# A hybrid layer with a PEER expert mixer: 160 gathered tokens instead of 128, and a down product with stationary weights and a transposed output

## The chip, the cores and the metric

The kernel runs on one core of a Trainium2 chip. A core has five engines that work side by side, each through its own queue of instructions: TensorE (PE) for matrix products, with the loading of its stationary operand shown apart (PEld); VectorE (DVE) and ScalarE (ACT) for elementwise work; GpSimd (POOL), here mostly the issuer of indirect gathers; and SyncE (SP), which issues most of the other transfers. Sixteen DMA engines move the data. The metric is the device time of one execution in microseconds (us); lower is better.

## The reference

One decoder layer on 512 tokens of width 2048, in float32. A mixer (gMLP and mLSTM heads behind one input projection) is added to x; the change does not touch it. Then comes the PEER mixer, in which each token picks 128 of 16384 experts (8 heads x 16), and a final norm:

```
h2 = rmsnorm(x, norm2_g)
qp = h2 @ peer_wq;  s1, s2 = scores of its two halves against 128 keys each
eidx, gate = top 16 of 16 x 16 candidate pairs, softmax, per head
act  = gelu(einsum("td,thkd->thk", h2, peer_u[eidx]))
x    = x + einsum("thk,thkd->td", gate * act, peer_v[eidx])
out  = rmsnorm(x, final_g)
```

## The kernel before

All large products are made from split operands: each float32 value becomes a high part `whi` or `Th` (rounded to fp32r) and a low part `wlo` or `Tl`, and `mm3` (lines 97 to 100) adds three matmuls, high x high, high x low, low x high. `split` (lines 68 to 70) makes the parts, the high one on ScalarE, the low one on VectorE.

The front, up to the last matmul of tile po at 699.8 us, is the mixer. After it, x with the mixer added goes to `x2d` in DRAM, the normed first 128 tokens go to `h2d`, and the normed, transposed activations of all tokens stand in `Th`, `Tl`.

The PEER mixer is computed in two ways at once:

- **The gathered path**, for tokens 0 to 127. `experts()` (line 543) gathers, for each of the 128 picks q, one row of `peer_u` per token (an indirect DMA into a tile `g`, three buffers, line 533), takes its dot product with the token's row `h20` on VectorE (line 548), then the gelu, and then gathers rows of `peer_v` and adds them, scaled, to `acc0` (line 557): 256 gathers of 128 x 2048 values.
- **The dense path**, for tokens 128 to 511. The *up stage* multiplies all 128 blocks of 128 experts by the 384 dense tokens (tile `pu`, line 698: weights stationary, the 384 tokens moving), takes the gelu and stores it as `Ad`. Meanwhile `combine()` (line 614) does the routing of the dense tokens and builds the combination matrix: per token, two one-hot matrices (lines 636 and 638, VectorE) are multiplied (line 639, TensorE, tile `pwb`, float32, each recorded as two matmuls), so that the gates stand at the places of the chosen experts. It is stored as `Wd` in 12 blocks of 32 tokens. The *down stage* goes through 16 groups of 8 expert blocks. `product(g)` loads `Ad` and `Wd` of a group, multiplies them and splits the result into `C`; then the activations of 128 tokens are stationary and 512 columns of `peer_v` move (line 748, tile `pv`): 4 column blocks `ch`, 3 token blocks, 8 expert blocks. `close` (line 751) adds each result to `acc`, which begins as x2.

The order of the work is set in four ways. The weights come in *pieces* of 128 x 1024, two from each 1 MB load on SyncE's queue, split three pieces ahead of their use (`LA = 3`); there are 256 pieces in each stage, 24 up matmuls or 18 down matmuls each. The gathers are handed out by `gather_step` (line 573): a fixed share is owed per piece (the 256 gathers over 466 slots, with 0.45 of the share while the first product is made and over the first 12 down pieces), and `fetch` adds a wait for the last matmul of a piece four back, so that gathers run at TensorE's pace. Units of routing and combination are handed out by a similar count (line 709). Last, the order on each engine's queue is not the order of writing: a scheduler with a model of the times of the instructions sets it when the program is built.

At the end, the last column block of the last group runs token block by token block: sums of squares, `rstd` (line 55), scaling, output (lines 763 to 776). The gathered tokens are finished beside the last group (lines 791 to 800).

Of the kernel before, what the change touches and what calls it, by code (L numbers as in the profile page):

```python
# [27 lines left out]
KP = KD // NP  # L28
TOPK = 16
# [6 lines left out]
def layer(ctx, tc, a, out, dbg=None):  # L36
# [18 lines left out]
    def rstd(dst, ssq, n):  # L55
        m = ssq.shape[-1]
        v = tiny.tile([P, 32], F32, tag="rs_v", name="rs_v")[:, :m]
        r = tiny.tile([P, 32], F32, tag="rs_r", name="rs_r")[:, :m]
        t = tiny.tile([P, 32], F32, tag="rs_t", name="rs_t")[:, :m]
# [362 lines left out]
    h2d = tc.dram_tile([P, D], F32, name="h2d")  # L422
    with ExitStack() as mx:
# [20 lines left out]
        hn = mid.tile([P, D], F32, name="hn")  # L444
        nc.vector.scalar_tensor_tensor(hn, xs[0], r2[:, 0:1], g2, op0=ALU.mult, op1=ALU.mult)
        nc.gpsimd.dma_start(h2d, hn)
# [6 lines left out]
    nc.gpsimd.dma_start(h20, h2d)  # L453
    sel0 = hg.tile([P, 3, P], F32, name="sel0")
    act = hg.tile([P, P], F32, name="act")
    rstack = ExitStack()
# [15 lines left out]
    done = [0]  # L472

    def route(t, heads=range(8), nb=4):
        s = slice(t * P, (t + 1) * P)
        for h0 in range(heads[0], heads[-1] + 1, nb):
# [36 lines left out]
            if t == 0:  # L513
# [3 lines left out]
                nc.vector.tensor_copy(eidx[:, r], ef)  # L517
                done[0] += nb * TOPK
# [7 lines left out]
            nc.vector.tensor_tensor(g3, g3, gs[:, :, None].to_broadcast(flat), op=ALU.mult)  # L526
            yield
# [4 lines left out]
    def fetch(table, q):  # L532
        g = hg.tile([P, D], F32, tag="g", name="g", bufs=3)
        i = nc.gpsimd.indirect_dma_start(out=g, out_offset=None, in_=table,  # L534
                                         in_offset=bass.IndirectOffsetOnAxis(ap=eidx[:, q:q + 1], axis=0))
# [5 lines left out]
    acc0 = []  # L541

    def experts():
        for q in range(P):
            while done[0] <= q:
                yield "wait"
            g = fetch(a["peer_u"], q)
            nc.vector.tensor_tensor_reduce(out=g, in0=h20, in1=g, op0=ALU.mult, op1=ALU.add, scale=1.0,  # L548
                                           scalar=0.0, accum_out=act[:, q:q + 1])
            yield "step"  # L550
        nc.scalar.activation(gate0, act, AF.Gelu_apprx_tanh)
        nc.vector.tensor_tensor(gate0, gate0, sels[0][:, 2, :], op=ALU.mult)
        acc0.append(hg.tile([P, D], F32, tag="h20", name="acc0"))
        nc.sync.dma_start(acc0[0], x2d[0])
        for q in range(P):
            g = fetch(a["peer_v"], q)
            nc.vector.scalar_tensor_tensor(acc0[0], g, gate0[:, q:q + 1], acc0[0], op0=ALU.mult, op1=ALU.add)  # L557
            yield "step"
# [176 lines left out]
    for g in range(NG):  # L735
        c = C[g % 2]
        nxt = product(g + 1) if g + 1 < NG else iter(())
        for ch in range(4):
# [50 lines left out]
            for t in range(3):  # L789
                close(t)  # L790
# [72 lines left out]
```

## Time and profile before

| | |
|---|---|
| median of 3 runs (lowest, highest) | 3072.26 us (3071.01, 3075.01) |
| the profiled execution: its span, first to last instruction | 3073.4 us |
| TensorE busy | 3046.3 us, 99% |
| VectorE busy | 2123.8 us, 69% |
| ScalarE busy | 1057.6 us, 34% |
| GpSimd busy | 413.0 us, 13% |
| up stage, first to last matmul | 815.3 to 1987.8 us |
| down stage, first to last matmul | 1987.9 to 3063.3 us |
| moved by DMA | 739.69 MB |

A row of a group names line, engine, operation, output <- inputs, shapes and count, then the busy time and the mean of one in ns, then how long the engine sat idle before it and what ended that. Matmuls overlap in the records, so their mean is not their price. A row of a tile gives minimum/median/maximum in ns and the first and last start. A row of a window gives busy time and count of each engine, the granted clock, the share of the DMA engines' time and GB/s. A row of the timeline gives start, length, engine, line and tile.

### The profile page before, as it was taken

Reading aid. Unit: us, or ns where it says so; the run is one execution under the profiler, and the core shown is the slowest. Engines: PE = TensorE matmul, PEld = TensorE weight load, DVE = VectorE, ACT = ScalarE, POOL = GpSimd, SP = SyncE. Lnnn points to the kernel's source line nnn. Section 1 sums busy time; section 2 is a strip of 40 time slices with the busy share of each in tenths; the row PEclk is TensorE's granted clock in tenths of the full one; section 3 lists DMA queues with packets and bytes.
Section 4 is the critical chain, followed back from the end, with each engine's and each line's share of the span. In section 5 each row is a group of like instructions: output and inputs, shape, how many; then the busy total and the mean of one; then the engine's idle time right before and its main releaser. Section 6 shows DMA issues by size and latency. Waiting matters only on the chain.

```text
span 3073.4 us, 38280 instructions
## 1 busy us (share of the span) xinstructions
PE 3046.3 (99%) x15181; PEld 2682.4 (87%) x15181; DVE 2123.8 (69%) x3431; ACT 1057.6 (34%) x1280; POOL 413.0 (13%) x299
## 2 busy tenths in 40 slices
PE   8999999999999999999999999999999999999998
PEld 7888888887899999999999999988888888878886
DVE  5534334224896898988888787577777787878764
ACT  5322335223332333334444444322222332222233
POOL 0000000000022121111111110021121232212100
PEclk9999999999999999999999999999999999999999
DMA  6223233334487787777777777889888888888853
GB/s 233 89 83 123 84 95 103 91 95 165 147 288 282 281 287 274 288 273 301 268 284 286 302 289 268 324 306 328 318 300 308 308 307 304 307 326 304 293 204 110
DMA packets 189652, 739.69 MB, mean 241 GB/s; under 512 B 13681, under 2 KB 38305, under 8 KB 136353
## 3 DMA queue, kind: packets, MB, share of 16 engines
q1 hardware_dynamic: 139456, 404.79, 37.9%
q0 software_dynamic: 40800, 307.29, 27.4%
q10 hardware_dynamic: 9216, 25.17, 2.1%
q8 instruction: 119, 1.95, 0.2%
q14 instruction: 61, 0.49, 0.0%
HBM read 677.43 MB, written 59.77 MB: 240 GB/s over the span
## 4 chain that ended last, share of the span: by engine, by line
PE 92%; issue 3%; DMA 2%; DVE 1%; ACT 0%; POOL 0%; SPq 0%; POOLq 0%; DVEq 0%; ACTq 0%
PE pu L100 11%; PE pu L99 11%; PE pu L98 11%; PE pv L100 10%; PE pv L98 10%; PE pv L99 10%; PE pn L98 4%; PE pn L99 4%; PE pn L100 4%; PE pwb L639 2%; PE po L100 2%; PE po L99 2%; PE po L98 2%; PE pw L100 1%; PE pw L98 1%
## 5 line engine op out<-in xcount | busy, mean ns | idle before, releaser
L69 ACT ACTIVATE whi<-raw 128x1024 fp32r<-128x1024 f32 x642 | 676.7, 1059 | 1607.9 <-PE pu L99 437.0
L70 DVE TENSOR_TENSOR wlo<-raw,whi 128x1024 fp32r<-128x1024 f32 x642 | 777.6, 1220 | 555.9 <-ACT whi L69 554.8
L98 PE MATMUL pu<-Th,whi 128*128 128x384 f32 x2048 | 704.2, 344 | 0.0
L100 PE MATMUL pu<-Th,wlo 128*128 128x384 f32 x2048 | 700.2, 342 | 0.1
L99 PE MATMUL pu<-Tl,whi 128*128 128x384 f32 x2048 | 700.1, 342 | 0.0
L100 PE MATMUL pv<-whi,C 128*128 128x512 f32 x1536 | 610.0, 397 | 0.0
L99 PE MATMUL pv<-wlo,C 128*128 128x512 f32 x1536 | 604.2, 393 | 0.2 <-DVE wlo L70 0.2
L98 PE MATMUL pv<-whi,C 128*128 128x512 f32 x1536 | 603.3, 394 | 0.0
L98 PEld LDWEIGHTS pu<-Th,whi 128*128 128x128 f32 x2048 | 386.1, 189 | 0.6
L99 PEld LDWEIGHTS pu<-Tl,whi 128*128 128x128 f32 x2048 | 386.0, 188 | 0.5
L100 PEld LDWEIGHTS pu<-Th,wlo 128*128 128x128 f32 x2048 | 386.0, 188 | 0.5 <-DVE wlo L70 0.5
L548 DVE CUSTOM_DVE_ANT_0 g<-h,g 128x2048 f32<-128x2048 f32 x128 | 292.9, 2288 | 132.0 <-DMA g<-in_peer_u,eidx 131.8
L557 DVE SCALAR_TENSOR_TENSOR acc<-g,gate,acc 128x2048 f32<-128x2048 f32 x128 | 300.6, 2348 | 114.6 <-DMA g<-in_peer_v,eidx 114.3
L99 PEld LDWEIGHTS pv<-wlo,C 128*128 128x128 f32 x1536 | 288.3, 188 | 73.6 <-DVE wlo L70 0.6
L100 PEld LDWEIGHTS pv<-whi,C 128*128 128x128 f32 x1536 | 288.3, 188 | 69.1
L98 PEld LDWEIGHTS pv<-whi,C 128*128 128x128 f32 x1536 | 288.3, 188 | 68.0
L534 POOL DMA_INDIRECT g<-in_peer_v,eidx x128 | 211.7, 1654 | 839.5 <-PE pv L100 630.0
L534 POOL DMA_INDIRECT g<-in_peer_u,eidx x128 | 180.8, 1413 | 913.2 <-PE pu L100 613.6
L99 PE MATMUL pn<-wlo,Th 128*128 128x512 f32 x512 | 204.2, 399 | 0.0
L100 PE MATMUL pn<-whi,Tl 128*128 128x512 f32 x512 | 203.0, 396 | 0.0
L98 PE MATMUL pn<-whi,Th 128*128 128x512 f32 x512 | 182.3, 398 | 0.0
L640 ACT ACTIVATE wst<-pwb 128x512 f32<-128x512 f32 x96 | 108.2, 1127 | 169.0 <-PE pwb L639 168.6
(255 smaller groups left out, 2932.1 us busy)
## 6 DMA issues: line engine op xcount, KB each, us to landing
raw<-in_u SPq DMA_DIRECT2D x128, 1024.0 KB
raw<-in_peer_v SPq DMA_DIRECT2D x128, 1024.0 KB
raw<-in_w_in SPq DMA_DIRECT2D x80, 512.0 KB
Ad<-ast ACTq DMA_DIRECT2D x64, 384.0 KB
Wd<-wst POOLq DMA_DIRECT2D x12, 2048.0 KB, 8.0
At<-Ad SPq DMA_DIRECT2D x32, 768.0 KB
Wt<-Wd SPq DMA_DIRECT2D x48, 512.0 KB
raw<-in_w_out SPq DMA_DIRECT2D x32, 512.0 KB
```

What stands on the lines that cost most here:

```text
L69: nc.scalar.activation(hi, src, AF.Copy)
L70: nc.vector.tensor_tensor(lo, src, hi.bitcast(F32), op=ALU.subtract)
L98: nc.tensor.matmul(o, sh, mh, start=start, stop=False)
L99: nc.tensor.matmul(o, sh, ml, start=False, stop=False)
L100: return nc.tensor.matmul(o, sl, mh, start=False, stop=stop)
L534: i = nc.gpsimd.indirect_dma_start(out=g, out_offset=None, in_=table, in_offset=bass.IndirectOffsetOnAxis(ap=eidx[:, q:q + 1], axis=0))
L548: nc.vector.tensor_tensor_reduce(out=g, in0=h20, in1=g, op0=ALU.mult, op1=ALU.add, scale=1.0, scalar=0.0, accum_out=act[:, q:q + 1])
L557: nc.vector.scalar_tensor_tensor(acc0[0], g, gate0[:, q:q + 1], acc0[0], op0=ALU.mult, op1=ALU.add)
L639: nc.tensor.matmul(pw[:, i * P:(i + 1) * P], o2, o1, start=True, stop=True)
L640: nc.scalar.activation(wst[:, :, f * 4:f * 4 + 4].rearrange("p i t -> p t i"), pw.rearrange("p (t i) -> p t i", t=4), AF.Copy)
```

## The change

Three parts:

- **Tokens.** 32 more tokens (128 to 159) take the gathered path; 352 stay dense (`TD`). Each of the 32 gets four partitions, each with 32 of its 128 picks, so that the 32 tokens take 32 + 32 further gathers of 128 rows, after the first 256. Their routing results are brought into this layout by 8 small copies on SyncE's queue, their rows by four loads into `h21`, which takes the buffer of `h20`; the sum of the first tile is stored to `y0d` meanwhile. At the end four float32 matmuls (`pick`) add the four partitions of a token. The combination matrix has 11 blocks.
- **Combination matrix.** The one-hot matrices are made four tokens at a time (two comparisons of 128 x 512), and the gate is put on by a ScalarE scaling per token, in place, ahead of its matmul.
- **Down product.** The weights are stationary, 128 columns of d at a time, and the 352 tokens move. The output is transposed (d on the partitions, `acc` is [128, 16, 352], and it begins empty). In the last group `settle` turns it back by TensorE transposes, adds x2, which is loaded late into `xf`, and does the final norm. `final_g` is loaded once, at the start of the stage.

The diff, cut to its core:

```diff
+G2 = 32
+S2 = P // G2
+TG = P + G2
+TD = T - TG
...
+        for t in range(2):
+            hn = mid.tile([P, D], F32, name="hn", bufs=2)
+            nc.vector.scalar_tensor_tensor(hn, xs[t], r2[:, t:t + 1], g2, op0=ALU.mult, op1=ALU.mult)
+            nc.gpsimd.dma_start(h2d[t], hn)
...
+            if t == 1:
+                for q in range(S2):
+                    c = q * G2 - r.start
+                    if 0 <= c < nb * TOPK:
+                        d = slice(q * G2, (q + 1) * G2)
+                        nc.sync.dma_start(eidx2[d, :], ei[0:G2, c:c + G2])
+                        nc.sync.dma_start(gate2[d, :], sels[t][0:G2, 2, d])
+                        done[1] += 1
...
     def experts():
+        for n, (ix, nq) in enumerate(((eidx, P), (eidx2, G2))):
+            if n == 0:
+                h = h20
+            else:
+                while done[1] < S2:
+                    yield "wait"
+                h = hg.tile([P, D], F32, tag="h20", name="h21")
+                for q in range(S2):
+                    nc.sync.dma_start(h[q * G2:(q + 1) * G2, :], h2d[1, 0:G2, :])
+            for q in range(nq):
...
+                g = fetch(a["peer_u"], ix, q)
+                nc.vector.tensor_tensor_reduce(out=g, in0=h, in1=g, op0=ALU.mult, op1=ALU.add, scale=1.0,
+                                               scalar=0.0, accum_out=act[:, q:q + 1])
+                yield "step"
...
+            acc = hg.tile([P, D], F32, tag="h20", name=f"acc{n}")
+            if n == 0:
+                nc.sync.dma_start(acc, x2d[0])
+            else:
+                nc.vector.memset(acc, 0.0)
+                nc.sync.dma_start(acc[0:G2, :], x2d[1, 0:G2, :])
+            for q in range(nq):
+                g = fetch(a["peer_v"], ix, q)
+                nc.vector.scalar_tensor_tensor(acc, g, gt[:, q:q + 1], acc, op0=ALU.mult, op1=ALU.add)
+                yield "step"
+            if n == 0:
+                nc.sync.dma_start(y0d, acc)
...
-    gathers = {"left": 2 * P, "slots": NP - 2 + NPC + nv - 24 - 28, "owed": 0.0}
+    gathers = {"left": 2 * P + 2 * G2, "slots": NP - 2 + NPC + nv - 24 - 28, "owed": 0.0}
...
+                        nc.vector.tensor_tensor(o1, io[:, None, :].to_broadcast(four),
+                                                sT[:, 0, c0:c0 + 4, None].to_broadcast(four), op=ALU.is_equal)
+                        nc.vector.tensor_tensor(o2, io[:, None, :].to_broadcast(four),
+                                                sT[:, 1, c0:c0 + 4, None].to_broadcast(four), op=ALU.is_equal)
                         for i in range(4):
-                            nc.vector.tensor_scalar(o1, io, sT[:, 0, c:c + 1], sT[:, 2, c:c + 1],
-                                                    op0=ALU.is_equal, op1=ALU.mult)
-                            nc.vector.tensor_scalar(o2, io, sT[:, 1, c:c + 1], None, op0=ALU.is_equal)
-                            nc.tensor.matmul(pw[:, i * P:(i + 1) * P], o2, o1, start=True, stop=True)
+                            nc.scalar.activation(o1[:, i, :], o1[:, i, :], AF.Copy, scale=sT[:, 2, c0 + i:c0 + i + 1])
+                            nc.tensor.matmul(pw[:, i * P:(i + 1) * P], o2[:, i, :], o1[:, i, :], start=True, stop=True)
...
-            last = mm3(pu, hi[:, c], lo[:, c], Th[:, k, P:], Tl[:, k, P:], k == 0, k == KD - 1)
+            last = mm3(pu, hi[:, c], lo[:, c], Th[:, k, TG:], Tl[:, k, TG:], k == 0, k == KD - 1)
...
+    def settle(ch, dbs, done):
+        for j, (t0, rows) in enumerate(toks):
+            o0 = t0 - TG
+            pt = bank(("mm", "sm")[ch % 2], f"pe{ch}_{j}_{dbs[0]}")
+            for db in dbs:
+                nc.tensor.transpose(pt[0:rows, db * P:(db + 1) * P], acc[:, 4 * ch + db, o0:o0 + rows], ident)
...
+            nc.vector.tensor_tensor(o, pt[0:rows, w], o, op=ALU.add)
...
-            po = [bank(("mm", "sm")[ch % 2], f"pv{g}_{ch}_{t}") for t in range(3)]
+            po = [bank(("mm", "sm")[ch % 2], f"pv{g}_{ch}_{db}")[:, 0:TD] for db in range(4)]
...
-                    r = mm3(po[t], c[:, 0, e, s], c[:, 1, e, s], hi[:, j], lo[:, j], e == 0, e == GE - 1)
+                    r = mm3(po[db], hi[:, j, s], lo[:, j, s], c[:, 0, e], c[:, 1, e], e == 0, e == GE - 1)
...
+            def close(db):
+                o = acc[:, 4 * ch + db, :]
+                if g == 0:
+                    nc.vector.tensor_copy(o, po[db])
+                else:
+                    nc.vector.tensor_tensor(o, po[db], o, op=ALU.add)
...
-                for t in range(3):
+                for db in range(4):
                     for pc in range(GE // 2):
-                        part(pc, t, *held[pc])
-                    close(t)
...
+                        part(pc, db, *held[pc])
+                    close(db)
+                settle(3, range(4), True)
                 continue
...
+            if g == NG - 1:
+                settle(ch, range(4), False)
...
+            pick = vp.tile([P, G2], F32, name="pick")
+            nc.vector.tensor_reduce(pick, ident.rearrange("p (s t) -> p t s", t=G2), axis=AX.X, op=ALU.add)
+            for ch in range(4):
+                d = slice(ch * 512, (ch + 1) * 512)
+                ph = bank(("mm", "sm")[ch % 2], f"ph{ch}")
+                nc.tensor.matmul(ph[0:G2, :], pick, y[:, d], start=True, stop=True)
+                nc.scalar.activation(y[0:G2, d], ph[0:G2, :], AF.Copy)
+            junk = hg.tile([P, D], F32, tag="g", name="junk", bufs=3)
+            finish(G2, y, junk, P)
+            y0 = hg.tile([P, D], F32, tag="g", name="y0", bufs=3)
+            nc.sync.dma_start(y0, y0d)
+            finish(P, y0, junk, 0)
```

More of the change, by code (lines that the diff above doesn't have):

```diff
@@ L539, in fetch @@
         return g
-    acc0 = []
+    acc2 = []
     def experts():
[L544 to L558, printed above, removed]
+        for n, (ix, nq) in enumerate(((eidx, P), (eidx2, G2))):
[8 more added lines that the diff above has]
+            for q in range(nq):
+                while n == 0 and done[0] <= q:
+                    yield "wait"
+                g = fetch(a["peer_u"], ix, q)
+                nc.vector.tensor_tensor_reduce(out=g, in0=h, in1=g, op0=ALU.mult, op1=ALU.add, scale=1.0,
+                                               scalar=0.0, accum_out=act[:, q:q + 1])
+                yield "step"
+            gt = (gate0, gate2)[n]
+            av = act[:, 0:nq]
+            nc.scalar.activation(av, av, AF.Gelu_apprx_tanh)
+            nc.vector.tensor_tensor(gt, av, sels[0][:, 2, :] if n == 0 else gate2, op=ALU.mult)
+            acc = hg.tile([P, D], F32, tag="h20", name=f"acc{n}")
[10 more added lines that the diff above has]
+                nc.sync.dma_start(y0d, acc)
+            else:
+                acc2.append(acc)
@@ L728, in layer @@
     C.append(tp.tile([P, 2, GE, TD], F32R, tag="Tl", name="C1"))
-    acc = tp.tile([P, NT, D], F32, tag="Th", name="acc")
+    top = tp.tile([P, KD * T], F32, tag="Th", name="top")
+    acc = top[:, 0:KD * TD].rearrange("p (k t) -> p k t", t=TD)
+    fg = top[:, KD * TD:KD * TD + D]
+    nc.sync.dma_start(fg, row_bc(a["final_g"], D))
+    toks = []
+    at = TG
+    while at < T:
+        toks.append((at, min(P - at % P, T - at)))
+        at += toks[-1][1]
     sq3 = vp.tile([P, 3, 4], F32, name="sq3")
@@ L781, in layer @@
                 hi, lo = queue.pop(0)
-                for t in range(3):
-                    last = part(pc, t, hi, lo)
+                for db in range(4):
+                    last = part(pc, db, hi, lo)
                 n += 1
@@ L788, in layer @@
                     advance(nxt, 1)
-            for t in range(3):
-                close(t)
+            for db in range(4):
+                close(db)
+            if g == NG - 1:
+                settle(ch, range(4), False)
         if g == NG - 2:
@@ L793, in layer @@
             advance(exps, 1)
-            fg = hg.tile([P, D], F32, tag="g", name="fg", bufs=3)
-            nc.sync.dma_start(fg, row_bc(a["final_g"], D))
-            y = hg.tile([P, D], F32, tag="g", name="y", bufs=3)
-            nc.scalar.activation(y, acc0[0], AF.Square, accum_out=ss3[:, 3:4])
-            rstd(r3[:, 3:4], ss3[:, 3:4], D)
-            nc.vector.scalar_tensor_tensor(y, acc0[0], r3[:, 3:4], fg, op0=ALU.mult, op1=ALU.mult)
-            nc.sync.dma_start(out[0:P, :], y)
+            y = acc2[0]
+            pick = vp.tile([P, G2], F32, name="pick")
[10 more added lines that the diff above has]
+            finish(P, y0, junk, 0)
+            xf += [hg.tile([P, D], F32, tag="g", name=f"xf{j}", bufs=3) for j in range(3)]
+            for j, (t0, rows) in enumerate(toks):
+                nc.sync.dma_start(xf[j][0:rows, :], x2d[t0 // P, t0 % P:t0 % P + rows, :])
     cpstack.close()
```

100 lines of the change are left out of this document (55 added, 45 removed).

## The prediction

> **What bounds the kernel now.** I read the page first, for the engine that never rests and for how full the transfers are; then busy time by window, to split the span into its two long stages; then the matmuls of each stage, for the time one of them takes; then the groups by shape, for what the change adds to VectorE and ScalarE.
>
> ```profile
> span 3073.4 us, 38280 instructions
> PE 3046.3 (99%) x15181; PEld 2682.4 (87%) x15181; DVE 2123.8 (69%) x3431; ACT 1057.6 (34%) x1280; POOL 413.0 (13%) x299
> GB/s 233 89 83 123 84 95 103 91 95 165 147 288 282 281 287 274 288 273 301 268 284 286 302 289 268 324 306 328 318 300 308 308 307 304 307 326 304 293 204 110
> 815.30:1987.90 1172.60, 1167.98 (x6965) 1165.33 (x6964) 964.15 (x2079) 461.31 (x537) 193.43 (x144) 1.00 0.78 284
> 1987.90:2950.00 962.10, 961.92 (x4124) 773.52 (x4123) 746.37 (x581) 281.42 (x260) 204.35 (x123) 1.00 0.86 308
> 1200.00:1300.00 100.00, 100.00 (x577) 99.79 (x576) 94.05 (x216) 35.53 (x45) 17.96 (x13) 1.00 0.78 285
> 1910.00:1920.00 10.00, 10.00 (x60) 10.00 (x59) 4.97 (x4) 2.50 (x3) 0.00 (x0) 1.00 1.02 422
> 2410.00:2420.00 10.00, 10.00 (x44) 8.04 (x43) 6.17 (x5) 2.12 (x2) 0.94 (x1) 1.00 1.03 395
> ```
>
> The window rows give start and end, then busy time of PE, PEld, DVE, ACT and POOL, the granted clock, the DMA share and GB/s. TensorE is busy throughout the up stage (815 to 1988, tile pu) and the down stage (1988 to 3063, tile pv) at full clock: it is the bound. The runners-up stand in the down stage: VectorE 746 of 962 us (78%), transfers at share 0.86 and 308 GB/s. VectorE at 94% (third window) did not stop TensorE.
>
> ```profile
> 1929.69 0.34 PE L98 MATMUL pu<-Th,whi 128*128 128x384 f32 x1
> 1939.91 0.34 PE L100 MATMUL pu<-Th,wlo 128*128 128x384 f32 x1
> L98 PE MATMUL pv<-whi,C x1536: 389/392/399, 1987.9 to 3062.9; 128*128 128x512 f32 x192
> L100 PE MATMUL pv<-whi,C x1536: 392/399/399, 1988.4 to 3063.3; 128*128 128x512 f32 x192
> L639 PEld LDWEIGHTS pwb<-o,o x768: 186/190/192, 1410.0 to 1906.1; 128*128 128x128 f32 x192
> 1609.38 0.61 PE L639 MATMUL pwb<-o,o 128*128 128x128 f32 x4
> 534.00 1.75 PE py L388 x16
> ```
>
> A matmul's recorded length (0.34 us) overlaps the next one, so its price is the step from start to start. The first two rows are the ends of 60 matmuls in a row: 10.22 us over 59 steps, 173.2 ns with 384 columns. The down stage's 4608 run from 1987.9 to 3063.3 without a gap: 1075.4 over 4607, 233.4 ns with 512.
>
> **The change part by part.** *Price of a 352-column matmul.* The trace has none. Neighbours: 384 columns 173.2, 512 columns 233.4, so 0.470 ns a column between them. Along that line 352 costs 158.2; in proportion to 384, 158.8. I take 158.6. Its far bounds are 173.2 (no gain below 384) and the 128-column pwb, four in 0.61 us with 0.27 each, so a step of 0.11 us. That row also speaks against a floor from the weight load: 128x128 loads, recorded at 190 ns, follow each other at 110.
>
> [...]
>
> *Up stage.* 128 experts x 16 blocks x 3 matmuls = 6144, each 14.6 ns less: -89.7. All of it is on TensorE's path.
>
> *Down stage.* Before, a group needs 4 column blocks x 3 token blocks x 8 x 3 matmuls, 4608 in all, 1075.5. After, 16 blocks x 8 x 3 per group, 6144 x 158.6 = 974.4: -101.1.
>
> *Combination matrix.* One of twelve blocks goes: 64 fewer pwb at 0.11, -7.0. VectorE loses 768 comparisons and gets 176 wide ones; ScalarE gets 352 scalings.
>
> ```profile
> L70 DVE TENSOR_TENSOR wlo<-raw,whi 128x1024 fp32r<-128x1024 f32 x642 | 777.6, 1220 | 555.9 <-ACT whi L69 554.8 <-issue 0.2
> L557 DVE SCALAR_TENSOR_TENSOR acc<-g,gate,acc 128x2048 f32<-128x2048 f32 x128 | 300.6, 2348 | 114.6 <-DMA g<-in_peer_v,eidx 114.3
> L548 DVE CUSTOM_DVE_ANT_0 g<-h,g 128x2048 f32<-128x2048 f32 x128 | 292.9, 2288 | 132.0 <-DMA g<-in_peer_u,eidx 131.8
> L636 DVE TENSOR_SCALAR o<-io,selT 128x128 f32<-128x128 f32 x384 | 133.4, 348 | 14.3 <-PE pwb L639 14.3
> L638 DVE TENSOR_SCALAR o<-io,selT 128x128 f32<-128x128 f32 x384 | 110.0, 287 | 0.0
> L753 DVE TENSOR_TENSOR acc<-pv,acc 128x512 f32<-128x512 f32 x192 | 125.9, 683 | 14.3 <-PE pv L100 14.2
> L664 DVE TENSOR_TENSOR At<-At,Wt 128x1536 f32<-128x1536 f32 x32 | 55.9, 1751 | 2.9 <-DMA Wt<-Wd 2.3 <-DMA At<-Ad 0.6
> L757 DVE TENSOR_TENSOR acc<-acc,fg 128x512 f32<-128x512 f32 x12 | 8.2, 687 | 3.2 <-ACT sj L755 3.2
> L356 ACT ACTIVATE cv<-vg 128x128 f32<-128x128 f32 x32 | 9.4, 296 | 0.0
> ```
>
> The wide comparisons, at the 0.687 of a 128x512 from SBUF, are 121 us where 243 were. The scalings, at the 0.296 of a 128x128 activation, are 104 us more on ScalarE, which works 461 of 1173 us there. But they stand between the comparison and the matmul: unhidden, a group of four waits 4 x 0.296 = 1.2 us, 88 groups 106 us; hidden, 0. They wait on ScalarE behind the split of the weights and the gelu, which follows the end of its matmuls; TensorE has other up matmuls to run meanwhile. I take +5.
>
> *Gathers.* 320 over the same 466 slots: 0.687 a piece instead of 0.549. Stepping the pacing code gives 133 gathers in the up stage and 123 in the down stage before (the x123 of the POOL column agrees), 167 and 153 after. In the up stage VectorE gets 34 x 2.29 = 78 more and loses 122; no charge. In the down stage they end at piece 229, and 229 pieces x 24 x 158.6 ns = 872 us, where 962 were. VectorE there: 746, +30 x 2.348 = +70; its additions out of PSUM are 4 x 0.517 where 3 x 0.683 were (1.04 ns an element from the 512 and 1536 rows), +1; the product an eleventh shorter, -8: 809 of 872, 93%, about the window that ran at 94%. Transfers: 308 x 962 = 296 MB, +30 gathers of 1.05 MB, -4 for narrower Ad and Wd, -3 for the load of x2 that goes: 321 MB, 368 GB/s. At 395 GB/s (the 2410 window) that takes 813 us and is hidden; at full share of the stage's own rate, 308/0.86 = 358, it takes 897, +25. Three pieces of look-ahead (11.4 us) take up short delays. I take +8.
>
> *SyncE's queue and the hand-overs.* SP now also carries 8 small copies of routing results, the store of the first tile's sum, four loads of the second tile's rows and one of its sum; the weight loads queue behind a waiting one.
>
> ```profile
> L534 POOL DMA_INDIRECT g<-in_peer_u,eidx x128: 932/1117/3646, 802.2 to 1884.0; - x128
> L534 POOL DMA_INDIRECT g<-in_peer_v,eidx x128: 932/1158/6837, 1904.3 to 2938.0; - x128
> DMA to landing us min/median/max: 5.5/7.0/16.4
> 2937.77 0.34 SPq L795 DMA_DIRECT2D fg<-in_final_g  x1
> 2943.45 13.89 SPq L87 DMA_DIRECT2D raw<-in_peer_v  x3
> 2960.59 0.36 SPq L800 DMA_DIRECT2D out<-y  x1
> ```
>
> The one hand-over of before, 20 us from the last u gather to the first v gather, left TensorE busy, and in the last three rows weight loads stand between a load and the store that needs it: the written order is not the queue's. Three hand-overs now: 0 to 5 us each; I take +3. GpSimd's queue gets 64 more issues at 1.1 us and a second store of normed rows ahead of the first gather; it works 204 of 962 us, so 0. The last group's output stores and reloads have the same cover and no gathers beside them.
>
> *The end.* 48 transposes at 0.11 (16 in 1.75) and four 512-column float32 sums, each two passes of 4 x 0.11: +5.3 and +3.5. TensorE waits for the last additions before each set of transposes, +1.
>
> ```profile
> 3063.34 0.40 PE L100 MATMUL pv<-whi,C 128*128 128x512 f32 x1
> 3063.77 0.69 DVE L753 TENSOR_TENSOR acc<-pv,acc 128x512 f32<-128x512 f32 x1 [0.58 <-PE pv L100]
> 3064.56 0.63 ACT L755 ACTIVATE sj<-acc 128x512 f32<-128x512 f32 x1 [0.97 <-DVE acc L753]
> 3065.31 0.69 DVE L757 TENSOR_TENSOR acc<-acc,fg 128x512 f32<-128x512 f32 x1 [0.85 <-ACT sj L755]
> 3067.50 1.15 ACT L773 ACTIVATE acc<-acc,r 128x1024 f32<-128x1024 f32 x1 [1.00 <-DVE r L66]
> ```
>
> Today only the last token block's chain is left after the last matmul, 10.1 us to the end. With d on the partitions all three token blocks end together: VectorE's part of a chain is some 3 us, so two more of them, +6 (3 to 10).
>
> *Sum.* 3073.4 - 89.7 - 101.1 - 7.0 + 8.8 + 1 + 6 + 3 + 5 + 8 = 2907.4. The span lies 1.1 above the median of the runs, 3072.26; so 2906.
>
> **The rivals.** *Transfers become the bound of the down stage.* For it: 368 GB/s on average where the page's best slice had 328, and a share of 0.86 that would pass 1. Against it: 395 and 422 GB/s over 10 us. Price in place of my 8: +25 at 358 GB/s, +107 if nothing beyond 328 can be held (979 us); 2923 to 3005. [...]
>
> *The scalings are not hidden:* +106 for 5, 3007. For it: they follow a wait for TensorE on ScalarE's queue. Against: only 461 of 1173 us taken.
>
> *A 352-column matmul pays for 384.* No gain in the up stage, 11 in the down stage (6144 x 173.2); crowding falls away: about 3078, no change. The pwb step of 0.11 speaks against it.
>
> *Slower: the ring of three gather buffers.* A buffer is held from issue to landing (7.0, at most 16.4) and 2.35 for VectorE. After, a gather is due every 872/153 = 5.7 us, so three buffers allow 17.1 us a turn against 9.4 at the median. Crowded transfers lengthen landings; beyond 17.1 the gathers set the pace, and VectorE, waiting in order, withholds the weights. The loss passes the 167 gained when a turn takes 20.4 us; at 21.5 the down stage takes 153 x 7.17 = 1096 and the kernel 3130. It needs the typical landing to be worse than the worst of before.
>
> **How the numbers follow.** Forecast 0.70 (own range 2875 to 2945), transfers 0.18, scalings 0.06, 352 as 384 0.03, ring 0.03. A difference of 0.2% is about what a measurement of this kernel can tell from none. All but the last two are faster: faster 0.94, same 0.03, slower 0.03. The range reaches from 2872 (no crowding, a matmul 1 ns cheaper) to 2975, which takes in half of the transfers' case.
>
> **What would show it.** Right: a step near 158.6 ns in both stages, the down stage's 6144 matmuls in about 985 us, VectorE above 90% there, TensorE without gaps over 1 us until the last group. Wrong: a step of 165 or more; TensorE gaps ended by VectorE's wlo, with gather landings over 15 us, in the down stage; pwb waiting for ScalarE by more than 20 us in total; more than 20 us after the last matmul of the down product.

## The result and the profile after

The changed kernel takes 2979.18 us (median of 4 runs, 2970.97 to 2981.29), the one before 3073.4 beside it; the ratio is 0.9689, interval 0.9675 to 0.9704. It is faster by 3.1%. The forecast was 2906 with a range to 2975: the sign is right, the gain is some 73 us smaller than forecast, and the time lies 4 us beyond the range. The profiled execution took 2980.17 us, its span is 2978.5.

These are lines of the page of the kernel after: busy times, GB/s in 40 slices, and the shares of the chain that ended last. A line that begins with L shows line, engine, operation, tiles, shapes and count, then busy time and mean ns, then idle time before it and what ended it.

```profile
span 2978.5 us, 41458 instructions
PE 2892.6 (97%) x16709; PEld 2724.1 (91%) x16709; DVE 2197.3 (74%) x3026; ACT 1127.3 (38%) x1632; POOL 530.9 (18%) x363
GB/s 240 85 85 125 86 91 103 91 95 181 106 302 354 325 327 309 322 318 340 305 347 363 328 335 362 311 336 361 357 349 356 363 339 352 368 349 338 344 191 142
PE 78%; DVE 11%; DMA 7%; issue 3%; ACT 1%; SPq 0%; ACTq 0%; DVEq 0%; POOLq 0%
L577 DVE CUSTOM_DVE_ANT_0 g<-h,g 128x2048 f32<-128x2048 f32 x160 | 364.7, 2282 | 37.7 <-DMA g<-in_peer_u,eidx 37.4
L592 DVE SCALAR_TENSOR_TENSOR acc<-g,gate,acc 128x2048 f32<-128x2048 f32 x160 | 375.1, 2345 | 18.1 <-DMA g<-in_peer_v,eidx 14.1
```

Before, TensorE was busy for 99% of the span. Now the chain, 92% TensorE before by its page, is 78% TensorE, with 11% VectorE and 7% transfers. The last two lines give a second sign: VectorE used to wait 131.8 and 114.3 us for gathers, now it waits 37.4 and 14.1. Much of its slack is gone.

The same kernel by windows (start and end, busy time of PE, PEld, DVE, ACT and POOL, granted clock, DMA share, GB/s): the whole down stage, a stretch of the up stage, and a stretch of the down stage.

```profile
1923.96:2960.40 1036.44, 1006.18 (x6188) 994.48 (x6188) 862.29 (x785) 311.51 (x314) 237.67 (x152) 0.99 0.89 327
1100.00:1300.00 200.00, 187.14 (x1134) 183.82 (x1134) 197.74 (x427) 67.41 (x88) 57.30 (x32) 0.98 0.86 313
2000.00:2700.00 700.00, 676.41 (x4162) 669.94 (x4161) 611.42 (x543) 204.06 (x196) 184.17 (x118) 0.99 0.96 354
```

In the second window VectorE is busy for 197.74 of 200 us, in the third the DMA engines are at 0.96. Before, the same two windows read 177.81 of 200 and 0.87, with TensorE busy throughout.

The waits of the kernel after name who stopped TensorE (in all, times, longest), and the last line what stopped ScalarE's split of the down weights:

```profile
PE pv L102 <- ACT whi L73: 18.5, 7, 5.0
PE pu L104 <- DVE wlo L74: 13.9, 5, 7.7
PE pv L104 <- DVE wlo L74: 11.6, 16, 2.2
PE pu L102 <- ACT whi L73: 11.0, 9, 1.8
ACT whi L73 <- DMA raw<-in_peer_v: 391.2, 70, 14.0
```

That is 24.9 us in the up stage and 30.1 in the down stage, all for weights that were not split in time. In the down stage five stops, 16.1 us together, stand behind single weight loads that took 15.0 to 16.9 us to land; the others are shorter and end with ScalarE's or VectorE's own order of work. One of the five, by the chain of waits between 2500 and 2523 us (start, length, what):

```profile
2501.82 15.87 DMA raw<-in_peer_v
...
2517.80 1.06 ACT whi L73
...
2518.91 0.43 PE pv L102
...
2520.23 0.29 PE pv L102
2520.52 0.29 PE pv L103
```

A weight load issued at 2501.82 lands 15.87 us later, ScalarE splits it, and TensorE starts again at 2518.91. A load holds two pieces, 2 x 24 x 0.160 = 7.7 us of matmuls, and there are two load buffers: a turn of issue, landing and splits has 15.4 us, and this landing alone takes more. A second loss follows: from 2520.2 the steps are 0.29 us instead of 0.16. The windows of the stop and of what follows show the granted clock falling from 0.98 to 0.50:

```profile
2516.50:2520.00 3.50, 1.09 (x6) 1.10 (x7) 1.12 (x1) 2.01 (x2) 0.69 (x1) 0.98 1.00 386
2519.97:2523.20 3.23, 3.23 (x13) 3.23 (x12) 3.23 (x3) 0.00 (x0) 0.00 (x0) 0.50 1.05 399
```

Here 3.2 us at half clock follow a stop of 4.13 us. Half clock also follows shorter stops (the granted clock is 0.50 from 2226.4 to 2229.7 us, behind a stop of 2.20 us), but not all of them (none behind the stop of 2.06 us that ends at 2090 us).

### The profile page after: what moved, and what is told of

Read it like the earlier page. It is cut to its first block, busy times and chain, and to the rows that moved or that the text cites. A ratio compares the mean times of both kernels' runs of the same rounds, so it can differ in the third digit from the quotient of the medians.

```text
span 2978.5 us, 41458 instructions
## 1 busy us (share of the span) xinstructions
PE 2892.6 (97%) x16709; PEld 2724.1 (91%) x16709; DVE 2197.3 (74%) x3026; ACT 1127.3 (38%) x1632; POOL 530.9 (18%) x363
## 4 chain that ended last, share of the span: by engine, by line
PE 78%; DVE 11%; DMA 7%; issue 3%; ACT 1%; SPq 0%; ACTq 0%; DVEq 0%; POOLq 0%
PE pu L104 9%; PE pu L102 9%; PE pu L103 9%; PE pv L104 8%; PE pv L102 8%; PE pv L103 8%; DMA raw<-in_peer_v 4%; PE pn L102 4%; PE pn L103 4%; PE pn L104 4%; DVE wlo L74 4%; PE pwb L681 3%; DVE g L577 2%; PE po L102 2%; PE po L104 2%
## 5 line engine op out<-in xcount | busy, mean ns | idle before, releaser
L73 ACT ACTIVATE whi<-raw 128x1024 fp32r<-128x1024 f32 x642 | 664.3, 1055 | 1371.2 <-DMA raw<-in_peer_v 391.2
L102 PE MATMUL pu<-Th,whi 128*128 128x352 f32 x2048 | 671.4, 328 | 11.0 <-ACT whi L73 11.0
L102 PE MATMUL pv<-C,whi 128*128 128x352 f32 x2048 | 663.9, 325 | 18.5 <-ACT whi L73 18.5
L104 PE MATMUL pu<-Th,wlo 128*128 128x352 f32 x2048 | 664.3, 326 | 13.9 <-DVE wlo L74 13.9
L103 PE MATMUL pu<-Tl,whi 128*128 128x352 f32 x2048 | 663.8, 324 | 0.0
L103 PE MATMUL pv<-C,whi 128*128 128x352 f32 x2048 | 663.2, 324 | 0.0
L104 PE MATMUL pv<-C,wlo 128*128 128x352 f32 x2048 | 599.1, 325 | 11.8 <-DVE wlo L74 11.6
L102 PEld LDWEIGHTS pv<-C,whi 128*128 128x128 f32 x2048 | 387.2, 189 | 21.7 <-ACT whi L73 20.8
L104 PEld LDWEIGHTS pu<-Th,wlo 128*128 128x128 f32 x2048 | 386.8, 189 | 15.7 <-DVE wlo L74 15.4
L554 POOL DMA_INDIRECT g<-in_peer_u,eidx x160 | 259.9, 1624 | 785.8 <-PE pu L104 298.1
L104 PEld LDWEIGHTS pv<-C,wlo 128*128 128x128 f32 x2048 | 376.3, 189 | 17.9 <-DVE wlo L74 17.0
L577 DVE CUSTOM_DVE_ANT_0 g<-h,g 128x2048 f32<-128x2048 f32 x160 | 364.7, 2282 | 37.7 <-DMA g<-in_peer_u,eidx 37.4
L592 DVE SCALAR_TENSOR_TENSOR acc<-g,gate,acc 128x2048 f32<-128x2048 f32 x160 | 375.1, 2345 | 18.1 <-DMA g<-in_peer_v,eidx 14.1
L103 PEld LDWEIGHTS pv<-C,whi 128*128 128x128 f32 x2048 | 387.2, 189 | 0.8 <-issue 0.8
L839 DVE TENSOR_TENSOR top<-pv,top 128x352 f32<-128x352 f32 x240 | 119.7, 518 | 71.9 <-PE pv L104 69.2
```

Of the source, the lines that this page charges most:

```text
L73: nc.scalar.activation(hi, src, AF.Copy)
L102: nc.tensor.matmul(o, sh, mh, start=start, stop=False)
L103: nc.tensor.matmul(o, sh, ml, start=False, stop=False)
L104: return nc.tensor.matmul(o, sl, mh, start=False, stop=stop)
L577: nc.vector.tensor_tensor_reduce(out=g, in0=h, in1=g, op0=ALU.mult, op1=ALU.add, scale=1.0, scalar=0.0, accum_out=act[:, q:q + 1])
L592: nc.vector.scalar_tensor_tensor(acc, g, gt[:, q:q + 1], acc, op0=ALU.mult, op1=ALU.add)
```

## The experiments

The theory after the result: TensorE's own time is as forecast but for the step, and the rest is weights split too late. Its rivals are VectorE being full, the DMA engines being full, the ScalarE scalings, the transposed product itself, and the handling of buffers. Stage lengths below run from the first to the last matmul of pu and of pv; after has 1109.3 and 1036.5 us, before 1172.4 and 1075.4. They come from one profiled execution of each kernel. Executions of one kernel lie up to 15 us apart (2960.34 to 2975.26 with rows of 8 KB), and the profiled one lies 8.2 us above the median of its kernel without VectorE work, and 5.9 below it with both buffers; so differences of about 5 us between stages are not shown.

### A fifth of the gathered path without its transfers, without its VectorE work, and without both

The first keeps the VectorE work on the tile that is already there:

```diff
-                g = fetch(a["peer_u"], ix, q)
+                g = fetch(a["peer_u"], ix, q) if q % 5 < 4 else g
...
-                g = fetch(a["peer_v"], ix, q)
+                g = fetch(a["peer_v"], ix, q) if q % 5 < 4 else g
```

> Every fifth gather (64 of 320, spread evenly over both stages) moves nothing; VectorE works on the tile of the gather before it, so its work stays and only the transfers go back to what they were before the change (about 256 MB of gathers). Leaves out part of the sum over the experts. The changed kernel takes 2979 us; its TensorE gaps over 0.4 us add up to 28 us in the up stage and 35 in the down stage, with another 10 to 15 of steps at half clock around them. Theory A (up stage held by VectorE, down stage by late weight loads): the down stage's gaps fall under 10 us, the up stage's stay above 20; 2935 to 2950. Theory B (VectorE in both): nothing changes, 2972 to 2985. Theory C (the transfers in both): both go, 2900 to 2915.

The second gathers, and leaves a fifth of the products out:

```diff
                 g = fetch(a["peer_u"], ix, q)
-                nc.vector.tensor_tensor_reduce(out=g, in0=h, in1=g, op0=ALU.mult, op1=ALU.add, scale=1.0,
-                                               scalar=0.0, accum_out=act[:, q:q + 1])
+                if q % 5 < 4:
+                    nc.vector.tensor_tensor_reduce(out=g, in0=h, in1=g, op0=ALU.mult, op1=ALU.add, scale=1.0,
+                                                   scalar=0.0, accum_out=act[:, q:q + 1])
...
+                if q % 5 < 4:
+                    nc.vector.scalar_tensor_tensor(acc, g, gt[:, q:q + 1], acc, op0=ALU.mult, op1=ALU.add)
```

> Every fifth gather is still moved but VectorE does nothing with it (64 operations of 2.3 us less, 147 us of VectorE). Leaves out the same part of the sum. Theory A: the up stage's gaps (28 us) fall under 8; the down stage keeps half or more of its 35; 2940 to 2955. Theory B: both go, 2900 to 2915. Theory C: nothing changes, 2972 to 2985.

The third has both lines of each pair under `if q % 5 < 4:`.

> Every fifth gather is left out, transfer and VectorE's work both, which leaves out the same part of the sum as the two runs before; 256 gathers as before the change, everything else as changed. The two alone gave 2953 (no transfer: the down stage's gaps fell from 35 to 12 us) and 2957 (no VectorE work: the up stage's from 28 to 19). If the added gathers are the whole cause: 2912 to 2930, gaps under 12 us in the up stage (8 of them the one at its start) and under 8 in the down stage. If shorter steps alone bring the waits (less time per piece for the weights): above 2940.

| | median us | ratio to before, interval | up stage | down stage |
|---|---|---|---|---|
| after | 2979.18 | 0.9689, 0.9675 to 0.9704 | 1109.3 | 1036.5 |
| no transfer for a fifth | 2952.79 | 0.9614, 0.9588 to 0.9640 | 1104.5 | 1007.3 |
| no VectorE work for a fifth | 2956.94 | 0.9618, 0.9601 to 0.9634 | 1096.2 | 1031.2 |
| neither | 2937.59 | 0.9548, 0.9527 to 0.9570 | 1093.3 | 1006.8 |

In the down stage the transfers count: without a fifth of them it is 29.2 us shorter, without the VectorE work 5.3, without both 29.7. In the up stage VectorE's work weighs more: 4.8, 13.1 and 16.0. There the two are not cleanly parted: TensorE's waits for weights fall from 24.9 us to 16.4 without the transfers, 18.1 without the VectorE work (I had set under 8 for that) and 7.6 without both, and the times of the first two runs lie 2 to 3 us above the ranges of the theory. With as many gathers as before the change, the third run takes 41.6 us less than after. That is between the two ranges that I had set: the added gathers are most of what the forecast missed, and not all of it. The windows of the second run (no VectorE work), the same stretches as above, fit that: TensorE still stops in the down stage, at an unchanged DMA share of 0.96 and with VectorE down to 564 of 700 us.

```profile
1100.00:1300.00 200.00, 191.66 (x1174) 189.00 (x1173) 195.92 (x453) 69.80 (x91) 54.74 (x34) 0.99 0.88 327
2000.00:2700.00 700.00, 678.42 (x4169) 672.33 (x4168) 564.03 (x512) 202.48 (x196) 179.05 (x119) 0.99 0.96 357
```

### The down weights in rows of 8 KB instead of 2 KB

The same bytes, laid out so that each load reads long rows:

```diff
-                    r = (g * GE + 4 * pc) * P
-                    yield from stream(a["peer_v"][r:r + 4 * P, ch * 512:(ch + 1) * 512]
-                                      .rearrange("(j p) d -> p j d", p=P), lambda r, i: r[:, 2 * i:2 * i + 2])
+                    yield from stream(a["vb"][g, ch, pc], lambda r, i: r[:, 2 * i:2 * i + 2])
...
+        "vb": A["peer_v"].reshape(16, 2, 4, P, 4, 512).transpose(0, 4, 1, 3, 2, 5),
```

> The down weights are laid out so that a 1 MB load has 8 KB in a row per partition, as the up weights have, instead of four rows of 2 KB; same bytes, same work. [...] Theory B: unchanged, 2972 to 2985. Theory C (only the amount of transfer counts): four packets of 84 ns against one of 309 save 8% of the weights' time; 5 to 10 us, 2965 to 2975.

2964.65 us, 0.9649 (0.9622 to 0.9677), its down stage 1023.3, 13.2 shorter. TensorE's waits for ScalarE there fall from 18.5 to 6.9 us, those for VectorE grow from 11.6 to 14.8. The lateness is a matter of transfers, and about half of what leaving a fifth of them out brings can be had by shaping them. Whether long rows land sooner beside the gathers or only take less of the DMA engines' time is not shown. Between 2000 and 2700 us of after a packet of 2 KB takes 84 ns and one of 8 KB 309 (medians), and four times 84 is 336; 2964.65 lies at the lower end of the 2965 to 2975 set for that saving alone.

### The down product alone

128 gathered tokens as before, with the new product and the new combination matrix: `G2 = 0`, and without the second tile.

> The down product and the combination matrix as changed, but 128 gathered tokens and 384 dense ones, as before the change. If a step costs what its columns cost: 6144 x 173.3 = 1065 us in the down stage against 1075, a few us back for the transposes and the longer end, no crowding: 3062 to 3078. If the transposed product has a cost of its own (four additions in place of three, transposes, stationary weights): over 3085.

3075.09 us, 1.0004 (0.9995 to 1.0014), down stage 1076.2: no difference. A row of its tile pv (minimum, median, maximum of one; first and last start):

```profile
L102 PE MATMUL pv<-C,whi x2048: 335/336/424, 1982.4 to 3058.3; 128*128 128x384 f32 x187
```

6144 matmuls of 384 columns take as long as 4608 of 512 (the settling included). What the turned product does is to let the dense tokens be any number; the gain comes only with fewer of them.

### 64 tokens more instead of 32

```diff
-G2 = 32
+G2 = 64
```

> 64 more tokens in place of 32 take the gathered path (384 gathers, 320 dense tokens, 10 blocks). A step should cost 146 to 147 ns; if TensorE alone set the time, 12288 x 13.3 = 163 us less, about 2825. By theory A the down stage would need 1.55 MB a piece in 3.5 us, 440 GB/s, where the changed kernel moves 354 at a DMA share of 0.96; held at about 358 a piece takes 4.3 us, and the up stage's VectorE, 95 to 100% busy, is asked for a fifth more gathers: 2990 to 3080, slower than with 32.

3044.86 us (3030.08 to 3071.43), 0.9910 (0.9880 to 0.9941): the second 32 tokens cost more than they save. A matmul of 320 columns is cheaper again (77 steps from 2015.70 to 2026.99, first lines below), but TensorE waits 100.7 us for up weights alone, and 52.2 in one stop for the sum of the gathers; the DMA engines stand at 0.99 (last line).

```profile
2015.70 0.31 PE L104 MATMUL pv<-C,wlo 128*128 128x320 f32 x1
...
2026.99 0.31 PE L102 MATMUL pv<-C,whi 128*128 128x320 f32 x1
```

```profile
PE pu L102 <- ACT whi L73: 56.6, 28, 6.8
PE ph L875 <- DVE acc L592: 52.2, 1, 52.2
PE pu L104 <- DVE wlo L74: 44.1, 29, 7.7
```

```profile
2000.00:2700.00 700.00, 648.92 (x4296) 634.79 (x4295) 628.25 (x595) 206.35 (x201) 200.42 (x128) 0.99 0.99 372
```

### The combination matrix as before

The one-hot matrices by 128 x 128 comparisons with the gate put on by VectorE, no scalings.

```diff
-                        nc.vector.tensor_tensor(o1, io[:, None, :].to_broadcast(four),
-                                                sT[:, 0, c0:c0 + 4, None].to_broadcast(four), op=ALU.is_equal)
...
-                            nc.scalar.activation(o1[:, i, :], o1[:, i, :], AF.Copy, scale=sT[:, 2, c0 + i:c0 + i + 1])
+                            nc.vector.tensor_scalar(o1, io, sT[:, 0, c:c + 1], sT[:, 2, c:c + 1],
+                                                    op0=ALU.is_equal, op1=ALU.mult)
```

> The changed kernel with the combination matrix made as before the change: 704 comparisons of 128x128 on VectorE (223 us) in place of 176 wide ones (121 us), no scalings on ScalarE. VectorE works 348 of 420 us in that part and would be asked for about 100 more: 3010 to 3050. If the scalings held TensorE up, it would be no slower: 2965 to 2985.

2979.20 us, 0.9688 (0.9673 to 0.9703): in sum this part of the change is worth nothing. It saves less than I had expected: VectorE is busy for 2248.4 us in this run and 2197.3 in after, 51 us and not 100, since neighbouring comparisons overlap in the records (before, one is recorded at 345 ns and the next starts 257 ns after its start). And from 1410 to 1830 us VectorE was not full: 379.20 of 420 us busy in this run (first line below) and 347.94 in after, TensorE busy throughout in both.

```profile
1410.00:1830.00 420.00, 420.00 (x2803) 420.00 (x2802) 379.20 (x758) 190.51 (x214) 101.58 (x70) 1.00 0.88 335
```

```profile
PE pv L102 <- ACT C L73: 10.2, 1, 10.2
```

The sum hides two things, each seen in one profiled execution. The up stage is 5 us shorter here (1104.3). But the last matmul of the combination matrix starts at 1903.3 us, where it is 1827.4 in after, so its last block is stored, and loaded again for the first product, too late, and TensorE waits 10.2 us between the two stages (second line). The time lies in the range that I had set for scalings that hold TensorE up, but in after TensorE waits for no scaling.

### More buffers in the down stage: for weights, for gathers, for both

If a load is late because it starts late, a third weight buffer should cure it:

```diff
+        W["n"] = W.get("n", 0) + 1
+        if "more" in W and W["n"] % 3 == 0:
+            raw = W["more"].tile([P, 2 * KP * 512], F32, tag="raw", name="raw", bufs=1)
+        else:
+            raw = W["pool"].tile([P, 2 * KP * 512], F32, tag="raw", name="raw", bufs=W["raw"])
...
     vp = pool(ctx, "vp")
+    W["more"] = vp
```

> The down stage gets a third 1 MB buffer for its weight loads (same transfers, same work), so that a load that takes 11 to 17 us is begun one load earlier. If the down stage waits because single loads are late: its gaps fall from 35 to under 15, 2950 to 2963. If it waits because the transfers are at their rate limit on average: unchanged, 2972 to 2985.

A fourth gather buffer is made in the same way in `fetch`, for every fourth gather of the down stage:

> The changed kernel with a fourth gather buffer in the down stage. If the ring of three buffers held the gathers, and they the rest: 2950 to 2968. If the transfers' rate is the limit: no faster, and one more gather in flight delays the weight loads: 2975 to 3000.

Both together (room for them comes from smaller scratch tiles and from keeping the picks and gates in the place of the routing results):

> The changed kernel with both a third weight buffer and a fourth gather buffer in the down stage; room for them is made by keeping small tables in place of others (no work changes). With the third weight buffer alone a gather was used 18.7 us after its issue (13.5 in the changed kernel) and VectorE 2.35 us later gave the buffer back, so three buffers give a gather each 7 us where 5.7 are needed; four would give one each 5.3. If the place in VectorE's queue and the ring of buffers is what is short: no gaps, no wait at the pick matmuls, 2940 to 2956. If the transfers' rate is short (0.96 of the DMA time in the changed kernel, 0.94 with the third buffer): waits of 30 us or more remain somewhere, 2970 to 3000.

| buffers for weights, gathers | median us | ratio, interval | down stage | TensorE's longest single wait there |
|---|---|---|---|---|
| 2, 3 (after) | 2979.18 | 0.9689, 0.9675 to 0.9704 | 1036.5 | 5.0 |
| 3, 3 | 3006.71 | 0.9765, 0.9745 to 0.9785 | 1058.9 | 65.7 |
| 2, 4 | 2981.99 | 0.9709, 0.9691 to 0.9727 | 1034.6 | 4.7 |
| 3, 4 | 2962.72 | 0.9647, 0.9633 to 0.9661 | 1015.8 | 2.4 |

I had expected the third weight buffer to bring 16 to 29 us or nothing. It made the kernel slower. Between 2000 and 2700 us TensorE never stops in it, as hoped (first line); but one wait of 65.7 us stands at the end (second line), for the sum of the gathers, and GpSimd waits for gather buffers (third line; 160.8 in after).

```profile
2000.00:2700.00 700.00, 700.00 (x4377) 700.00 (x4376) 594.41 (x536) 220.23 (x204) 144.23 (x102) 1.00 0.94 340
```

```profile
PE ph L880 <- DVE acc L596: 65.7, 1, 65.7
...
POOL g L558 <- DVE acc L596: 250.6, 44, 18.0
```

The gathers are not slow to land. From the records of the DMA packets, a gather of the down stage (2200 to 2600 us) lands 8.1 us after its issue on the mean in after and 7.8 here; but its product starts 13.5 us after the issue in after and 18.7 here. A landed gather waits behind what stands ahead of its product on VectorE, as in the third weight buffer's timeline:

```profile
2407.72 2.35 DVE L596 SCALAR_TENSOR_TENSOR acc<-g,gate,acc 128x2048 f32<-128x2048 f32 x1
2414.74 1.63 DVE L74 TENSOR_TENSOR C<-At,C 128x1408 fp32r<-128x1408 f32 x1 [4.67 <-ACT C L73]
2416.28 1.22 DVE L74 TENSOR_TENSOR wlo<-raw,whi 128x1024 fp32r<-128x1024 f32 x1
2417.41 2.35 DVE L596 SCALAR_TENSOR_TENSOR acc<-g,gate,acc 128x2048 f32<-128x2048 f32 x1
```

Here VectorE stands idle for 4.67 us for the split of C, then does two splits, and only then the next product. A turn of a buffer is 18.7 + 2.35 = 21 us, three buffers give a gather each 7.0 us, and one is due each 5.7: the gathers fall behind and end late, with nothing beside them. A fourth buffer alone changes nothing, since gathers were not late there (14.0 us from issue to use in 2200 to 2600). With both, a turn of 21.3 + 2.35 us is shared by four: one each 5.9 us; the wait at the end is gone, and the split of the down weights hardly waits for a load any more, 50.3 us where it was 391.2:

```profile
ACT whi L73 <- DMA raw<-in_peer_v: 50.3, 10, 12.2
...
PE pv L106 <- ACT whi L73: 14.5, 6, 2.4
...
PE pv L108 <- DVE wlo L74: 6.5, 9, 1.7
```

So 20.7 us of the down stage in the profiled executions (the medians differ by 16.5) were a matter of when loads may start and how many gathers may be under way, not of bytes. Nor do the weight loads land sooner: by the DMA packets they take 7.8 us on the mean in after and 8.0 here, and 14 and 15 of the 128 take over 11.4 us. I had set 2940 to 2956 for that theory and 2970 to 3000 for a bound by rate; 2962.72 lies between them: the waits decide for the first, and its price was set too high. What is left are short stops of 2.7 us such as this chain: ScalarE waits for the last matmul of the group before it may write the next C, and the split of the weights stands behind that.

```profile
2425.95 0.17 PE pv L108
...
2426.14 1.39 ACT C L73
...
2427.58 1.51 issue
2429.09 1.23 DVE wlo L74
...
2430.36 0.43 PE pv L108
```

The rows of 8 KB on top of both buffers:

> The same with 8 KB rows for the down weights. If the ring was short, the rows now add nothing or a few us: 2936 to 2956. If the transfers' rate is short, they save 8% of the weights' time: 10 to 15 us less than the run without them.

2962.80 us, 0.9639 (0.9626 to 0.9652), down stage 1018.8: nothing is added. That fits that long rows and an early start cure the same lateness.

### Three that missed

The late gathers of the third weight buffer can be approached in other ways. All three runs keep that buffer. With rows of 8 KB and gathers dealt out more evenly (shares of 0.94, 1.2 and 0.96 in `gather_step`):

> The changed kernel with 8 KB rows for the down weights, the third weight buffer in the down stage, and gathers dealt out by time rather than by piece (0.94 of the share a piece while VectorE routes, 1.2 while the combination matrix is made, where VectorE is 83% busy, 0.96 in the down stage). Theory A: gaps of the up stage from 28 to under 20, of the down stage from 35 to under 12: 2930 to 2950. If the third buffer and the rows do nothing together: 2960 to 2970 as with the rows alone.

3010.53 us, 0.9779 (0.9762 to 0.9796), where I had set 2930 to 2950. The up stage grew to 1138.9 us. TensorE stops for 8 us in 1410 to 1830 (the line below, of this run), where it is busy throughout in after, and for 14.5 us from there to 1953. A wait of 42.5 us for the gathers' sum remained in the down stage.

```profile
1410.00:1830.00 420.00, 411.91 (x2733) 409.29 (x2732) 345.83 (x352) 280.90 (x550) 103.13 (x75) 0.99 0.88 340
```

Handing the gathers out differently moved stops into the up stage and did not bring their end forward: the last product ends at 2920.4 us, with the third buffer alone at 2916.7. The next two have the finish of the gathered tokens behind the third column block of the last group, the x2 rows in buffers of their own. The first of them has the rows of 8 KB as well:

> Third weight buffer, 8 KB rows for the down weights, and the finish of the gathered tokens (the pick matmuls and what follows) moved 12 pieces later, into the last group; x2 for the dense tokens is loaded into buffers of the product instead of the gathers'. With the third buffer alone the down stage had no gaps but one of 66 us, TensorE waiting for the last gathers at the pick matmuls (43 us with the rows and another dealing). 12 pieces are 46 us. If only the place of that wait was wrong: down stage about 1000 to 1010 us, total 2935 to 2955. If the transfers cost the same wherever they are waited for: 2960 to 2985.

The same without the long rows:

> The same without the 8 KB rows (2 KB rows as in the changed kernel). The wait at the pick matmuls should be the 66 us less 46: 2950 to 2970. If the transfers cost the same wherever they are waited for: 2972 to 2990.

2985.22 us, 0.9700 (0.9685 to 0.9715), and 2983.17, 0.9703 (0.9690 to 0.9716). A wait of some 44 us stays; it only moved:

```profile
PE ph L879 <- DVE acc L596: 44.6, 1, 44.6
```

The gathers were late by their buffers, and no place for the finish makes them earlier. In both runs their last product even ends some 28 us later than with the third buffer alone (2944.9 us); why is not known.

## Why the prediction was wrong

Forecast span 2907.4, measured 2978.5: 71.1 us, of which the up stage has 28.5 (1109.3 for 1080.8), the down stage 41.4 (1036.5 for 995.1), the end 2.0 (18.1 for 16.1), and -0.8 lies ahead of the stages. TensorE as the bound and the gain from fewer columns were right; three terms of the sum were not.

**The step of a 352-column matmul: mis-sized, 17.2 us.** I took 158.6 ns. These two rows of the down stage of after are 76 steps apart, 12.15 us, 159.9 ns; all undisturbed steps of both stages give 160.0:

```profile
2049.76 0.32 PE L103 MATMUL pv<-C,whi 128*128 128x352 f32 x1
...
2061.91 0.32 PE L102 MATMUL pv<-C,whi 128*128 128x352 f32 x1
```

1.4 ns x 12288 = 17.2. The 320 columns of the experiment give 11.29 us / 77 = 146.6, so 320, 352 and 384 lie on a line of 0.416 ns a column (173.2 - 146.6 over 64). My line was drawn from 384 to 512, across two products; at 0.416 ns a column their steps of 173.2 and 233.4 ns would leave 13.5 and 20.4 ns beside the columns, an estimate, since the slope of the second was not measured. From the 384 columns down that slope gives 159.9 for 352, and the sum would have been 2922, still 57 us short.

**"In the up stage VectorE gets 34 x 2.29 = 78 more and loses 122; no charge": failed, some 25 us** (the 19.9 that the step leaves of the stage's 28.5, and the 5 set aside for the scalings, which cost nothing). The 122 are not there. I added up recorded lengths, 133.4 + 110.0 us, of comparisons that overlap: one is recorded at 345 ns, and the next starts 257 ns later. VectorE was busy with the comparisons for 185.0 us before and 112.9 after, 72 less, which only balances the 78. These rows are windows of the tile `o`, before (PE, PEld, DVE) and after (PE, PEld, DVE, ACT):

```profile
815.00:1987.00 1172.00, 142.26 (x768) 135.42 (x768) 184.99 (x768) 1.00 0.78 285
815.00:1987.00 1172.00, 93.30 (x704) 90.00 (x704) 112.94 (x176) 110.83 (x352) 0.99 0.88 328
```

So VectorE is busy for 964 us of the up stage before and 972 after, in a stage that is 63 us shorter. And I set a sum over the stage against a sum. What is saved is saved from 1410 us on, where there was room; the gathers are added from 815 us on, where routing already kept VectorE at 512 of 595 us. There it now works 569 (before and after, all five engines):

```profile
815.00:1410.00 595.00, 591.08 (x3370) 589.15 (x3369) 512.40 (x1087) 207.41 (x262) 119.55 (x77) 1.00 0.78 281
815.00:1410.00 595.00, 570.34 (x3500) 565.23 (x3500) 568.75 (x1147) 210.53 (x276) 167.06 (x100) 0.99 0.87 322
```

From 1100 to 1300 us it is full (197.74 of 200), the splits come late, and TensorE waits. How much of that is VectorE's work and how much the transfers of the added gathers, the runs without a fifth part only roughly. The largest single stop is the first, 7.7 us up to 822.8, in the chain of after:

```profile
806.47 7.96 DMA g<-in_peer_u,eidx
...
814.44 2.29 DVE g L577
...
821.62 1.14 DVE wlo L74
...
822.80 0.66 PE pu L104
```

With a larger share per piece the second gather is issued at 806.47 instead of 812.87 us, its product gets a place ahead of the first weight split on VectorE, and the split waits for it and for the routing behind it. Only 3 us of this stop are new. Before, too, the first low part came late: its first matmul started 5.3 us after the first of the stage, as it does in the run with 128 gathered tokens, and in after 8.3 us.

**"I take +8" for the crowding of the down stage: mis-sized, some 35 us.** From the starts of all its matmuls, intervals that exceed a step by over 0.4 us add up to 34.7 us, and smaller excesses, most of them at half clock, to 12.9: 47.6, where the sum had 8 and 4 more for hand-overs and settling. The transposes and sums took 5.9 us, 2.9 less than their 8.8. With 8.6 for the step, 47.6 - 12 - 2.9 + 8.6 is the 41.4 within a microsecond. The likely case already held 93% for VectorE (87% was measured up to the last gathered product, 797 of 918 us), but what decides the longest stops is when a weight load lands: "three pieces of look-ahead (11.4 us) take up short delays" was right, and landings of 15.0 to 16.9 us are not short. My rival "transfers become the bound" came nearest in size (+25 at 358 GB/s, the 308 of the stage over its share of 0.86), but it is not shown as told: 372 GB/s were held over 700 us with 64 more tokens, and with two more buffers the same bytes cost 20.7 us less. The ring of three gather buffers, given 0.03, did not occur in after; it is real all the same, and set the pace as soon as a weight buffer was added, at a turn of 21 us, not by late landings but by VectorE's order of work. (A slip without effect: the lower end of the range, 2872, is not what its two parts give, 2906 - 8 - 12.3 = 2886.)

**Right.** TensorE's own time: fewer columns are the whole gain, and the product turned alone gives none. The scalings are hidden (+5 for nothing: pwb waited for ScalarE nowhere; they cost 391 ns each, not 296). The addition of 128 x 352 out of PSUM takes 518 ns where 517 was worked out. The end takes 18.1 us after the last matmul of the down product for 16.1. The signs that I named for "wrong" were half right: TensorE's stops are ended by wlo and whi, but the gathers land in 8.1 us (7.8 before, 2200 to 2600 us of both), not over 15; it is single weight loads that take over 15.

What stays open: how the two kinds of transfers share the DMA engines, that is, why some weight loads take 16 us beside gathers and most about 8. Rows of 8 KB help, but no run measures that share by itself.

## What to carry to other kernels

Work that moves from a full engine to engines with slack is paid where the slack is, not on the average: set it against the windows in which it will run, one by one, and take an engine's time from the busy time of a window, not from recorded lengths that may overlap. When a second engine or the DMA engines are close to full, look at each ring of buffers as a turn (issue, landing, place in the consumer's queue, use) divided by its length, and think of all rings that the same engine serves, since one more buffer in a single ring can slow the others, as the third weight buffer did here (3006.71 us for 2979.18). And take the step of a matmul from a neighbour of the same form, since a line through another form can miss by 1%, which was 17 us here.

## What the runs showed of the hardware

- Steps at full clock: 146.6 ns for 320 columns (pv with 64 more tokens), 160.0 for 352 (pu and pv of after), 173.2 for 384 (pu of before): 0.416 ns a column and 13.5 ns more.
- A stop of TensorE of 4.13 us was followed by 3.2 us at a granted clock of 0.50, with steps of 0.29 us: half of that, 1.6 us, comes on top of the stop. A stop of 2.20 us was followed by half clock too, one of 2.06 us was not.
- One core moved 372 GB/s over 700 us at a DMA share of 0.99, with gathers and weight loads mixed; over 10 us 422 (before) and 413 (with 64 more tokens) were seen.
- Two comparisons of 128 x 128 on VectorE are recorded at 345 and 283 ns, and the second starts 257 ns after the first: 768 of them keep it busy for 185.0 us, not for the 243 that the recorded lengths add up to.
